# The last four hidden pairs of a feed-forward block by seven block products instead of eight

## The chip, the cores and the metric

The kernel runs on one core of one Trainium2 chip. TensorE (PE) multiplies, VectorE (DVE), ScalarE (ACT) and GpSimd (POOL) work on tiles, SyncE's queue (SP) issues the loads and stores. The metric is the device time of one execution, in microseconds; the time before is the median of three runs.

## The reference

One inference step of an encoder trunk of two layers over 512 prompt frames and 8 x 16 sample frames (640 tokens), width 1024, hidden width 2816, all in float32. Layer 0 is a convolution module and a SwiGLU feed-forward block; layer 1 is banded attention with a shared key/value and a second feed-forward block. The change is in the feed-forward block of layer 0:

```python
def swiglu_ffn(h, g, w_in, w_out):
    a, b = jnp.split(rms_norm(h, g) @ w_in, 2, axis=-1)
    return h + (jax.nn.silu(a) * b) @ w_out
```

The convolution module that comes before it is: RMSNorm, pointwise layer with a gate, causal depthwise convolution of width 31, LayerNorm over the channels, SiLU, pointwise layer (`w_pw2`), added to h.

## The kernel before

**Number format.** Matrix products run in a reduced float32 format in three passes. Every operand is split into `hi` (a ScalarE copy into the reduced format) and `lo` (the remainder, a subtraction), and `mm3` adds `wh*xh + wl*xh + wh*xl` in PSUM, three matmuls for each block of 128 rows. `wsplit` loads a weight tile of up to 128 x 2048 through SP's queue into `raw`, makes `whi` on ScalarE (L156), and `wlo` (L160) on VectorE and GpSimd: its argument `pool` says how many quarters of it GpSimd makes. `raw`, `whi` and `wlo` have two buffers each; every third load has a third raw buffer, `rx`, as long as the pool of that name is open. `xsplit` (L165, L166) splits the moving operand, ScalarE then VectorE.

**Layout.** Activations lie with the features on the partitions: `h` is 128 x 8 x 640. The tokens are in two groups: group 0 has 256 (128 samples and the first 128 prompt frames), group 1 has 384. The hidden width is 22 blocks of 128; a *pair* j is the a-part and the b-part of one of them: `ffn_in` takes 8 blocks x 3 matmuls for each part, 48 matmuls of 256 columns (group 0) or 384 (group 1), then the gate (L293, L294 for group 0, whose input has been normalised beforehand; L296 to L299 for group 1, whose input is only scaled by the gain, with 1/rms, `bca`, multiplied in behind the product), and the split of the hidden rows. `ffn_out` multiplies the hidden rows of a chunk of pairs by `w_out` and adds the result into `h` (L309). With 5 to 8 pairs in the chunk it takes two output tiles to one weight load; with 4 or fewer, four tiles, and it makes all its weights before the first tile. PSUM has four banks for all this (`mm`, L93).

**Order.** Engines work in order; the order of the instructions in each queue is set at build time by a scheduler that simulates the program with priorities (`tc.high_priority` puts splits and gates ahead). For the convolution module the order is written by hand in `PLAN`, a list of steps. Those that matter here: `d101 d127` (VectorE convolves four channel blocks of group 1), `n1` (`conv_ln(1)`, LayerNorm of group 1: column sums by additions on GpSimd, L201, sums over partitions by tiny matmuls, L210, spread again by matmuls, L222), `f` (one chunk of pairs for group 0, as work for PE during the convolution of group 1: chunks 0-5, 6-11, 12-17, with three quarters of each `wlo` on GpSimd), `w1` (the second pointwise layer of group 1, `pw2`), `r1` (`rms_late`: RMSNorm of group 1 for the feed-forward block). After the plan come pairs 18 to 21 for both groups together (`FC`), then pairs 0 to 17 for group 1 (`FD`), and then the attention stage, whose first act is the RMSNorm of `h` for keys and queries.

**The second block.** The feed-forward block of layer 1 computes pairs 3 to 21 by seven block products. The 1024 input features are cut in two halves and the 640 tokens in two halves of 320 (`TH`); the a- and b-weights of a pair then make a 2 x 2 block matrix, and the 2 x 2 product is computed with seven products of blocks (a Strassen-Winograd scheme) instead of eight. A `Unit` is one such pair: `prep` loads and splits four weight blocks and three sums of them (L165/L166, sums at L922, two on VectorE and two on GpSimd, then `prep_back` into `bk`), `m1` to `m7` are the products (`prod`, 12 matmuls of 320 columns each, L977), with additions between them; `xc` holds the seven token blocks (B11, B21, B22 and the sums T1 to T4), split, made once. Units overlap: the next unit's `m1`, `m5`, `m6`, `m2` alternate with this one's `m7`, `m3`, `m4`.

## Time and profile before

| | |
|---|---|
| median of 3 runs | 1541.64 us (1540.84 to 1542.74) |
| profiled execution | 1541.31 us, of which the span of the trace is 1539.5 |
| busy share of the span | PE 95%, VectorE 68%, ScalarE 43%, GpSimd 29% |
| granted TensorE clock, mean | 0.988 |
| data moved | 200.54 MB, mean 130 GB/s |

The profile is of one execution, taken by the hardware profiler. Times in it are us from the span's start. A row of the timeline has start, length, engine, line of the kernel, operation, output<-input, shape and count, and in brackets how long the engine was idle before it and what ended that. A row of grouped instructions has count, total busy time, mean ns of one, and the idle time before them with what ended it. The busy time of a matmul overlaps that of the next: the distance between starts, not the mean of one, is what a matmul costs. PEld is TensorE's weight load, beside the matmuls.

### The profile page before, as it was taken

What the parts mean: (1) busy time and instruction counts of PE and PEld (TensorE: products, weight loads), DVE (VectorE), ACT (ScalarE), POOL (GpSimd) and SP (SyncE); (2) the same over time, 40 slices, a digit from 0 to 9 for tenths busy, and PEclk for the clock granted to TensorE, in tenths of its full rate; (3) what the DMA queues carried; (4) which work ended last, traced back from release to release, by engine and by line L of the source; (5) the groups of instructions that cost most, each with busy time, mean ns of one, the idle gap of its engine ahead of it and who ended that gap; (6) DMA issues with size and microseconds to landing.
All of it is one profiled execution on the core that took longest, in us unless ns stands there. A gap on an engine that the chain in (4) does not pass through costs nothing.

```text
span 1539.5 us, 27212 instructions
## 1 busy us (share of the span) xinstructions
PE 1467.9 (95%) x11054; PEld 1397.9 (91%) x11054; DVE 1049.0 (68%) x1890; ACT 667.1 (43%) x1196; POOL 447.3 (29%) x406
## 2 busy tenths in 40 slices
PE   5988898989999999999999999999999999999998
PEld 5878878988999999999988798896989999999998
DVE  6994999989555444556577767666796467467456
ACT  4544455545423323235455445343564144244144
POOL 6965458987401000001322111110421011011010
PEclk9989899999999999999999999999999999999999
DMA  7884334454421333432555545444103222222222
GB/s 261 249 219 143 123 103 162 146 183 151 151 83 56 123 123 123 126 120 96 196 184 195 170 151 199 150 158 151 32 25 117 76 83 89 76 83 90 76 83 83
DMA packets 57022, 200.54 MB, mean 130 GB/s; under 512 B 10176, under 2 KB 20672, under 8 KB 44096
## 3 DMA queue, kind: packets, MB, share of 16 engines
q1 hardware_dynamic: 56608, 198.48, 39.1%
q8 instruction: 87, 1.43, 0.4%
q10 hardware_dynamic: 288, 0.31, 0.1%
q14 instruction: 39, 0.32, 0.1%
HBM read 187.55 MB, written 11.22 MB: 129 GB/s over the span
## 4 chain that ended last, share of the span: by engine, by line
PE 73%; DVE 15%; issue 3%; ACT 3%; POOL 3%; DMA 3%; SPq 0%; POOLq 0%; ACTq 0%; DVEq 0%
PE mm L176 13%; PE mm L177 13%; PE mm L178 13%; PE pb L977 6%; DVE w L443 4%; PE pc L977 4%; DVE wlo L160 4%; PE pa L977 3%; PE w L803 1%; PE pb L176 1%; PE pb L178 1%; PE pb L177 1%; PE pa L178 1%; PE pa L176 1%; PE pa L177 1%
## 5 line engine op out<-in xcount | busy, mean ns | idle before, releaser
L177 PE MATMUL mm<-x,wlo 128*128 128x256 f32 (+1 forms) x1344 | 417.8, 313 | 15.8 <-DVE wlo L160 15.4
L176 PE MATMUL mm<-x,whi 128*128 128x256 f32 (+1 forms) x1344 | 414.4, 312 | 9.2 <-ACT x L165 6.9
L178 PE MATMUL mm<-x,whi 128*128 128x256 f32 (+1 forms) x1344 | 413.0, 311 | 2.5 <-DVE x L166 2.5
L177 PEld LDWEIGHTS mm<-x,wlo 128*128 128x128 f32 x1344 | 257.1, 191 | 19.4 <-DVE wlo L160 18.3
L176 PEld LDWEIGHTS mm<-x,whi 128*128 128x128 f32 x1344 | 255.1, 191 | 14.1 <-ACT x L165 7.7
L178 PEld LDWEIGHTS mm<-x,whi 128*128 128x128 f32 x1344 | 255.3, 191 | 5.2 <-DVE x L166 4.1
L156 ACT ACTIVATE whi<-raw 128x2048 fp32r<-128x2048 f32 (+2 forms) x87 | 143.9, 1658 | 171.9 <-PE mm L178 105.1
L160 DVE TENSOR_TENSOR wlo<-raw,whi 128x2048 fp32r<-128x2048 f32 (+5 forms) x87 | 156.4, 1801 | 44.7 <-ACT whi L156 44.0
L922 POOL TENSOR_TENSOR raw<-raw 128x512 f32<-128x512 f32 x38 | 56.4, 1485 | 326.4 <-DVE raw L922 255.2
L177 PE MATMUL mm<-hid,wlo 128*128 128x256 f32 (+1 forms) x352 | 107.6, 308 | 6.1 <-DVE wlo L160 6.1
L160 POOL TENSOR_TENSOR wlo<-raw,whi 128x1536 fp32r<-128x1536 f32 (+3 forms) x33 | 93.0, 2822 | 55.1 <-ACT whi L156 55.1
L178 PE MATMUL mm<-hid,whi 128*128 128x256 f32 (+1 forms) x352 | 105.8, 307 | 0.8 <-DVE hid L166 0.7
L443 DVE SCALAR_TENSOR_TENSOR w<-gp,dwv,w 128x384 f32<-128x384 f32 x180 | 104.4, 613 | 0.9
L176 PE MATMUL mm<-hid,whi 128*128 128x256 f32 (+1 forms) x352 | 104.4, 307 | 0.0
L201 POOL TENSOR_TENSOR acc<-sq,sq 128x384 f32<-128x384 f32 (+1 forms) x8 | 8.1, 1006 | 255.8 <-ACT sq L185 255.8
L156 ACT ACTIVATE whi<-rx 128x2048 fp32r<-128x2048 f32 (+1 forms) x30 | 54.0, 1800 | 54.0 <-PE mm L178 42.0
L177 PEld LDWEIGHTS mm<-hid,wlo 128*128 128x128 f32 x352 | 66.0, 188 | 7.1 <-DVE wlo L160 7.1
L160 DVE TENSOR_TENSOR wlo<-rx,whi 128x2048 fp32r<-128x2048 f32 (+4 forms) x30 | 62.9, 2098 | 13.3 <-ACT whi L156 12.4
L423 POOL TENSOR_TENSOR y<-y,cvt 128x256 f32<-128x256 f32 (+1 forms) x60 | 67.9, 1132 | 4.3 <-ACT cvt L422 2.2
L178 PEld LDWEIGHTS mm<-hid,whi 128*128 128x128 f32 x352 | 65.7, 188 | 1.2 <-DVE hid L166 1.2
L176 PEld LDWEIGHTS mm<-hid,whi 128*128 128x128 f32 x352 | 65.1, 188 | 0.3 <-ACT hid L165 0.3
L165 ACT ACTIVATE whi<-raw 128x1024 fp32r<-128x1024 f32 x38 | 39.4, 1054 | 54.2 <-DVE raw L922 19.1
(329 smaller groups left out, 3648.2 us busy)
## 6 DMA issues: line engine op xcount, KB each, us to landing
raw<-in_w_in SPq DMA_DIRECT2D x49, 1024.0 KB
raw<-in_w_out SPq DMA_DIRECT2D x28, 768.0 KB
cache<-in_ck SPq DMA_DIRECT2D x32, 512.0 KB
cache<-in_cv SPq DMA_DIRECT2D x32, 512.0 KB
raw<-in_w_pw SPq DMA_DIRECT2D x14, 1024.0 KB
rx<-in_w_in SPq DMA_DIRECT2D x13, 1024.0 KB
rx<-in_w_pw SPq DMA_DIRECT2D x8, 1024.0 KB
raw<-in_w_kq SPq DMA_DIRECT2D x8, 1024.0 KB
```

Source lines behind the costliest of these rows:

```text
L156: nc.scalar.activation(out=hi[:, a:b], in_=raw[:, a:b], func=AF.Copy)
L160: eng.tensor_tensor(out=lo[:, a:b], in0=raw[:, a:b], in1=hi[:, a:b].bitcast(F32), op=ALU.subtract)
L165: nc.scalar.activation(out=hi, in_=src, func=AF.Copy)
L176: nc.tensor.matmul(ps, wh, xh, start=(i == 0), stop=False)
L177: nc.tensor.matmul(ps, wl, xh, start=False, stop=False)
L178: nc.tensor.matmul(ps, wh, xl, start=False, stop=(i == last))
L201: last["acc"] = eng.tensor_tensor(out=acc[:, :n], in0=prev, in1=s(), op=ALU.add)
L423: nc.gpsimd.tensor_tensor(out=y[g][:, c, :], in0=y[g][:, c, :], in1=pr[:, :n], op=ALU.add)
L443: nc.vector.scalar_tensor_tensor(out=dst, in0=src, scalar=wj, in1=dst, op0=ALU.mult, op1=ALU.add)
L803: nc.tensor.matmul(st[32 * b:32 * b + 32, 0:512], qv[b], KC[b // 2][:, b % 2, :], start=True, stop=True)
L922: ENG[e].tensor_tensor(out=out, in0=a, in1=b, op=op)
L977: nc.tensor.matmul(ps, a[:, c], b[:, k, :], start=(first and k == 0 and i == 0), stop=(k == 3 and i == 2), skip_group_check=not first)
```

## The change

- `FS`, group 0's chunks, become 0-5, 6-11, 12-16 and pair 17 alone. `PLAN` still has three `f`, so pair 17 follows after the plan, and `r1` leaves the plan: `rms_late(1)` is called behind it, and pair 17 of group 0 after it, with three quarters of `wlo` on GpSimd (`PFB` = 3). The three-buffer raw pool (`rxs`) closes before that.
- `rms_late(1, ..., keep=xg)` keeps the scaled rows of group 1 in a tile of their own, `xg`.
- `LE`: the additions of `conv_ln(1)`, for mean and variance, go from GpSimd to VectorE.
- Group 1's pairs 0-5, then the token blocks, then its pairs 6-17, all with `PFB` = 3 (before: `wlo` on VectorE alone). The blocks are made from `xg` in pieces of one feature block (256, 384 or 320 columns): VectorE adds and multiplies, `xsplit` for B11, T1, T2, B21, T3; B22 and T4 are split whole once group 1's operand buffer is free.
- Pairs 18 to 21 come last, for all tokens, as four `Unit`s in one chunk, with the same code as the second block; in this stage their PSUM tiles come from the four `mm` banks in turn. Then `ffn_out` for both groups.
- `Unit`, `prod`, `bank`, `tmp` and the loop (`units`) move up in the file and take the weight source as an argument; the host reorders the b-weights of pairs 18 to 21 as it does for layer 1. A `hook` argument of `ffn` is added and not used by the plan.

```diff
-FS = ((0, 6), (6, 6), (12, 6))
+FS = ((0, 6), (6, 6), (12, 5), (17, 1))
+CHC = 5
-PLAN = ("a0 y ... s1 d101 d127 n1 f f w1 r1")
+PLAN = ("a0 y ... s1 d101 d127 n1 f f w1")
...
-    def rms_late(g, gain, engs=SQ, cut=CUT):
+    def rms_late(g, gain, engs=SQ, cut=CUT, keep=None):
...
-                t = tp.tile([P, 384], F32, tag="n1", name=nm("n1"), bufs=NB1)
+                t = (tp.tile([P, 384], F32, tag="n1", name=nm("n1"), bufs=NB1) if keep is None
+                     else keep[:, k, GR[g][0]:GR[g][0] + n])
...
+    def bank(tag=None):
+        if stage[0] == 0:
+            return mmt()
...
+    LE = (nc.gpsimd, nc.vector)
...
-        r, v = colmean(mu, [lambda c=c: y[g][:, c, :] for c in order], n, LCUT, "mst")
+        r, v = colmean(mu, [lambda c=c: y[g][:, c, :] for c in order], n, LCUT, "mst", LE[g])
...
-        bc, _ = rstd_bc([y[g][:, c, :] for c in order], n)
+        bc, _ = rstd_bc([y[g][:, c, :] for c in order], n, eng=LE[g])
...
-    xs0, xs1 = late[0], late[1]
     cv.close()
+    rxs.close()
+    third[1] = None
...
+    xs0, xs1 = late[0], rms_late(1, V_NFFN, keep=xg)
+    ffn({0: hp0}, w_in0, w_out0, {0: xs0}, (0,), chunks, PFB)
+    hid0.close()
     hid1 = ExitStack()
     hp1 = hid1.enter_context(tc.tile_pool(name="hp1", bufs=1))
-    ffn({0: hp0}, w_in0, w_out0, {0: xs0}, (0,), chunks, PFB)
-    if FC:
-        ffn({0: hp0, 1: hp1}, w_in0, w_out0, {0: xs0, 1: xs1}, (0, 1), FC)
-    ffn({1: hp1}, w_in0, w_out0, {1: xs1}, (1,), FD)
...
+    ffn({1: hp1}, w_in0, w_out0, {1: xs1}, (1,), FD[:1], PFB)
+    for k in range(KT):
+        add("v", xg[:, k, 0:256], xs0[0][:, k, :].bitcast(F32), xs0[1][:, k, :].bitcast(F32))
+        add("v", xg[:, k, 256:640], xg[:, k, 256:640], bca[:, 256:640], ALU.mult)
...
+    def put4(i, src):
+        for k in range(4):
+            xsplit(src[:, k, :], xc[i][0][:, k, :], xc[i][1][:, k, :])
+
+    def sub4(out, a, b):
+        for k in range(4):
+            add("v", out[:, k, :], a[:, k, :], b[:, k, :], ALU.subtract)
+
+    put4(B11, b11)
+    sub4(tq, b12, b11)
+    put4(T1, tq)
+    sub4(tq, b22, tq)
+    put4(T2, tq)
+    put4(B21, b21)
+    sub4(b12, b22, b12)
+    put4(T3, b12)
+    sub4(tq, b21, tq)
+    ffn({1: hp1}, w_in0, w_out0, {1: xs1}, (1,), FD[1:], PFB)
     hid1.close()
...
+    u = Unit(w_in0, FC[0][0], hids[0], 0)
+    u.prep((a22[:, 0:512], a22[:, 512:1024]))
+    with tc.high_priority(offset=HP):
+        put(B22, b22)
+        put(T4, tq)
+    xgs.close()
...
+    u.prep_back()
+    for f in (u.m1, u.m5, u.m6, u.m2):
+        f()
...
+    units(w_in0, range(FC[0][0], FT), pairs(FC), FC, u, hids, hid_c, outs0)
```

More of the change, by code (lines that the diff above doesn't have):

```diff
@@ new lines, in tmp, with add, copy, prod @@
+    def tmp(t):
+        if stage[0] == 0 and t == "t3":
+            t = "n1"
+        return tp.tile([P, 384], F32, tag=t, name=nm(t))[:, 0:HT]
+    def add(e, out, a, b, op=ALU.add):
+        ENG[e].tensor_tensor(out=out, in0=a, in1=b, op=op)
+    def copy(out, src):
+        nc.scalar.activation(out=out, in_=src, func=AF.Copy)
+    def prod(ps, w, x, first):
+        wh, wl = w
+        xh, xl = x
+        for k in range(4):
+            c = slice(k * P, (k + 1) * P)
+            for i, (a, b) in enumerate(((wh, xh), (wl, xh), (wh, xl))):
+                nc.tensor.matmul(ps, a[:, c], b[:, k, :], start=(first and k == 0 and i == 0),
+                                 stop=(k == 3 and i == 2), skip_group_check=not first)
@@ new lines, in put, with units @@
+    def put(i, src):
+        xsplit(src, *xc[i])
+    def units(src, js, where, chunks, u, hids, new_hid, outs):
+        for j in js:
+            c, jj = where[j]
+            w = None
+            if j + 1 < FT:
+                w = Unit(src, j + 1, hids[c], where[j + 1][1])
+                w.prep()
+                w.m1()
+            u.m7()
+            if w:
+                w.m5()
+            u.m3()
+            u.m4()
+            if w:
+                w.m6()
+                w.m2()
+            if jj == chunks[c][1] - 1:
+                outs(c)
+                if w:
+                    hids.append(new_hid())
+                    w.hid = hids[-1]
+            u = w
@@ L339, in tile_trunk, with pairs @@
+    def pairs(chunks):
+        return {j0 + jj: (c, jj) for c, (j0, ch) in enumerate(chunks) for jj in range(ch)}
     hid0 = ExitStack()
@@ L524, in step, with hook @@
     def step(op, arg):
+        if op == "f":
+            def hook(jj):
+                for t in arg.split("."):
+                    if t and int(t[0]) == jj:
+                        step(t[1], t[2:])
+            ffn({0: hp0}, w_in0, w_out0, {0: late[0]}, (0,), (chunks.pop(0),), PFA, hook=hook)
+            return
         g, cs = int(arg[:1] or 0), [int(c) for c in arg[1:]]
@@ L898, in tile_trunk @@
     xg = [xg[:, 0:4], xg[:, 4:8]]
[L899 to L907 removed]
+    stage[0] = 1
     proj_o(NP // 2 - 1)
@@ L1185, in tile_trunk @@
         put(T4, tq)
-    where = {}
-    for c, (j0, ch) in enumerate(F1):
-        for jj in range(ch):
-            where[j0 + jj] = c, jj
     xgs.close()
```

260 lines of the change are left out of this document (127 added, 133 removed).

## The prediction

> **What bounds the kernel now.** I read the page's busy shares first, then a table by stage, then the waits and rows inside the stages that the change touches.
>
> ```profile
> span 1539.5 us, 27212 instructions
> ...
> PE 1467.9 (95%) x11054; PEld 1397.9 (91%) x11054; DVE 1049.0 (68%) x1890; ACT 667.1 (43%) x1196; POOL 447.3 (29%) x406
> ```
>
> Seen over the span PE is the bound. The table by stage (columns: stretch, its length, busy time and count of PE, PEld, DVE, ACT, POOL, then clock, DMA share, GB/s) says where it isn't:
>
> ```profile
> 327.00:386.00 59.00, 53.77 (x463) 52.97 (x463) 50.30 (x56) 29.84 (x40) 46.46 (x22) 1.00 0.48 161
> 386.00:420.00 34.00, 34.00 (x197) 33.74 (x196) 16.64 (x22) 14.94 (x19) 18.01 (x9) 1.00 0.45 155
> ...
> 504.00:730.00 226.00, 225.72 (x1305) 225.40 (x1303) 119.37 (x147) 78.40 (x97) 7.04 (x6) 1.00 0.35 118
> 1349.00:1463.00 114.00, 114.00 (x858) 113.63 (x858) 70.64 (x101) 41.82 (x64) 15.55 (x12) 1.00 0.25 83
> ```
>
> From 207 to 386 three chunks of group 0 (18 pairs) fill PE while VectorE convolves group 1; PE idles for 5.2 of the last chunk's 59 us. From 386 to 730 PE is full: second pointwise layer of group 1 (to 420), the four shared pairs (to 476), their output (to 504), group 1's eighteen pairs (to 730). The last row is a stretch of the second feed-forward block, which already works by seven products, with PE full too. So a microsecond of PE work saved after 386 is a microsecond of time; one moved from before 386 to after it isn't free.
>
> **The saving: four pairs by seven products.** The first two rows are from the chain of waits in the second block (start, length, what), the other two start a group-0 half of successive shared pairs in the timeline:
>
> ```profile
> 1385.05 2.33 PE pa L977 x15
> ...
> 1397.48 2.33 PE pa L977 x15
> ```
>
> ```profile
> 448.93 0.28 PE L176 MATMUL mm<-x,whi 128*128 128x256 f32 x1
> ...
> 462.69 0.28 PE L176 MATMUL mm<-x,whi 128*128 128x256 f32 x1
> ```
>
> A shared pair takes 462.69-448.93 = 13.76 us (48 matmuls of 256 columns and 48 of 384). A unit takes 1397.48-1385.05 = 12.43 us (84 of 320). 4 x 1.33 = 5.3 us gained. The Trainium skill ("TensorE: Matmul & The Clock Gate", section "Wait — 56ns, not 53.3ns?") gives a matmul of N columns N / 2.4 GHz + 2.5 ns; by it the estimate would be 13.04 us a pair, 11.41 us a unit, 6.5 us in all. I stay with the rows, which show the units 1.0 us slower than that.
>
> Per unit VectorE and ScalarE do more than per pair (3584 columns split instead of 2048, four block sums of the weights, two of them on POOL), hidden behind PE in the second block, whose last row above has DVE 62% busy and PE full. The output after the four pairs (476 to 504) is the same work.
>
> **The pair moved back.** Chunk three shrinks from six pairs to five. Its PE work, 48 matmuls of about 0.1135 us (13.76 us less 48 of 226/1305 = 0.173, over 48) plus 24 for its output, is 8.2 us; it comes again after the pointwise layer. What the chunk loses to waiting (5.2 us) goes down by a sixth: about 1.0 us gained. But PE now reaches the pointwise layer 8.2 us earlier, near 378, and its input must be there:
>
> ```profile
> 332.82 3.46 POOL L201 TENSOR_TENSOR acc<-acc,y 128x384 f32<-128x384 f32 x3 [0.16 <-ACT y L446]
> ...
> 349.40 1.03 POOL L201 TENSOR_TENSOR acc<-sq,sq 128x384 f32<-128x384 f32 x1 [1.85 <-ACT sq L185]
> 351.21 3.48 POOL L160 TENSOR_TENSOR wlo<-rx,whi 128x1536 fp32r<-128x1536 f32 x1 [0.78 <-ACT whi L156]
> ...
> 366.36 2.28 POOL L201 TENSOR_TENSOR acc<-acc,sq 128x384 f32<-128x384 f32 x2
> ```
>
> ```profile
> 344.11 3.72 DVE L166 TENSOR_TENSOR hid<-t,hid 128x256 fp32r<-128x256 f32 x1
> ...
> 381.97 1.02 DVE L166 TENSOR_TENSOR x<-n,x 128x384 fp32r<-128x384 f32 x2
> ...
> 393.97 1.03 DVE L166 TENSOR_TENSOR x<-n,x 128x384 fp32r<-128x384 f32 x2 [1.32 <-ACT x L165]
> ```
>
> The normalised group 1 arrives in eight pieces from 383 to 395. The sum of squares before it lasts from 349.4 to 368.6 on POOL, 19.2 us, because four splits like the 3.48 us one stand between seven additions. On VectorE (LE) seven additions at 0.54 (the split of the same shape, half of 1.02-1.03) are 3.8 us, plus waits. VectorE's 128x256 subtraction took 3.72 us where POOL was inside a split (a free one, below, 0.42). With two such waits of 3.5 the sum lasts about 11 us, 8 less than before; the mean's last three additions go the same way (3 x 0.54 for 3.46) and give about 2 more. 10 against the 8.2 needed: no new wait, but no slack. Ends: 2 us gained more, 5 us of waiting (below).
>
> The Trainium skill ("SBUF — State Buffer", section "SBUF: two separate sides") calls the port pair of VectorE and GpSimd an exclusive lock, which a VectorE operation with two SBUF inputs and a GpSimd operation hold against each other for the whole instruction. The 3.72 us row agrees. It speaks against both LE and splitting by POOL during group 1's pairs; my sum has it in as two waits.
>
> **What the moved pair costs where it lands.** It is a chunk of its own: pair 17, then eight output tiles of three matmuls. Weight halves whi/wlo have two buffers. In order of use: pair 17 takes A, output weights of tiles 0-3 B, of 4-7 A, group 1's first pair B. So that pair's weights can be split only when tiles 0-3 are done, and these need the hidden rows of pair 17.
>
> ```profile
> 441.69 0.41 DVE L294 TENSOR_TENSOR t<-t,mm 128x256 f32<-128x256 f32 x1
> 442.59 0.42 DVE L166 TENSOR_TENSOR hid<-t,hid 128x256 fp32r<-128x256 f32 x1 [0.48 <-ACT hid L165]
> ```
>
> ```profile
> L156 ACT ACTIVATE whi<-raw 128x2048 fp32r<-128x2048 f32 x51 | 97.6, 1914 | 98.7 <-PE mm L178 80.9 <-PE pb L178 5.9 <-issue 4.1
> ...
> L160 POOL TENSOR_TENSOR wlo<-raw,whi 128x1536 fp32r<-128x1536 f32 x12 | 43.6, 3634 | 18.0 <-ACT whi L156 18.0
> ```
>
> ```profile
> 343.50 0.69 DVE L160 TENSOR_TENSOR wlo<-raw,whi 128x512 fp32r<-128x512 f32 x1 [1.51 <-ACT whi L156]
> ```
>
> The group of whole-tile splits shows that they wait for PE to free the buffer (80.9 of 98.7 us idle before them). After pair 17's last matmul the hidden rows take 443.01-441.69 = 1.3 us, with 0.1 to hand over 1.4, in which PE has no other work. Then tiles 0-3 (12 x 0.1135 = 1.4), the split (1.91, first quarter on VectorE 0.69, 0.4 of hand-overs) against tiles 4-7 (1.4): 1.6 more. I take 3.0 us lost. Ends: nothing, if hidden rows and weights overlap what is left of the layer before; 6.3, if VectorE's quarter has to wait for POOL's 3.63 us part, as in chunk three:
>
> ```profile
> 326.92 0.39 PE L176 MATMUL mm<-x,whi 128*128 128x256 f32 x2
> 329.17 0.38 PE L177 MATMUL mm<-x,wlo 128*128 128x256 f32 x1 [1.86 <-DVE wlo L160]
> ```
>
> **Group 1's pairs.** Splits go three quarters to POOL (3.63 us, after 1.91 on ACT: 5.6 of the 8.3 us that a pair, 48 x 0.173, gives). Into VectorE's idle time (107 of 226 us) go the token blocks: 16 additions and products of 256 or 384 columns, 16 differences and 20 splits of 320, about 0.5 each, 26 us, then two splits of 1280; ScalarE's 20 copies are as short. They are hidden unless a gate of the last pair of a chunk stands behind a blocked one: 0.5 us over three chunks; ends 0 and 6 (three waits of 3.5 less what other tiles cover). The third raw buffer is closed before these pairs. SP's load of 1 MB is short enough for two: issued at 391.79, its transfer ends by 396.
>
> ```profile
> 391.79 0.33 SPq L145 DMA_DIRECT2D raw<-in_w_in  x1
> ```
>
> ```profile
> 394.00:396.00 2.00, 2.00 (x13) 2.00 (x12) 1.00 (x2) 0.35 (x1) 0.00 (x0) 1.00 0.96 406
> ```
>
> **Entering and leaving the units.** The first unit's weights get their buffer 36 x 0.173 = 6.2 us before PE ends group 1; the chain split, three sums (one on POOL), split is longer. The same start in the second block:
>
> ```profile
> 1139.51 0.38 PE L977 MATMUL pa<-x0f,whi 128*128 128x320 f32 x1 [1.22 <-DVE t L922]
> ...
> 1148.46 0.41 PE L977 MATMUL pc<-x1f,wlo 128*128 128x320 f32 x1 [1.27 <-DVE wlo L166]
> ```
>
> There the blocks were late too; here all but two are long made. I take 1.0; ends 0 and 3.8 (those two and smaller ones). Accumulators come from four banks instead of six; each is read out at least 12 matmuls (1.8 us) before its next use, so nothing. At the end, group 0's last additions now come 16 us (96 matmuls of 0.173) before the next stage, not over 200, so its split and squares share ScalarE and VectorE with the next weights. That entry now costs
>
> ```profile
> 731.02 0.36 PE L176 MATMUL mm<-x,whi 128*128 128x256 f32 x1 [1.30 <-DVE h L309]
> ```
>
> and I add 0.5; ends 0 and 3. Eight more additions into h are hidden.
>
> **Sum.** -5.3 -1.0 +3.0 +0.5 +1.0 +0.5 = -1.3. The profiled execution took 1541.31 (span 1539.5 and 1.8 around it), 0.33 under the median: 1540.0 us, no measurable change (0.2%, about 3.1 us, is what a measurement of this kernel can tell).
>
> **Rivals.**
> - Faster. The waits where the moved pair lands are covered, and the shorter sum of squares takes another 1 us of chunk three's stalls: -5.3 -2.0 +0.8 +0.5+0.5 = -5.5, 1535.8 us. For it: PE took partial tiles of several outputs in the pointwise layer without a stall. Against: with three matmuls to a tile there are no partial tiles. 0.37.
> - Slower, by the port lock as the skill's rule would have it, worked from rows: every one of the four POOL splits between 349 and 369 holds an addition of the chain up for some 3.3 us, the sum lasts 3.8+13 = 17 us, 2 less than before, the mean gives 1.5, and PE, 8.2 us early, waits 4.7 us more: 1544.7 us. It decides once fewer than about 6 us are won on the chain. Against: VectorE often enters first (the 0.69 us row). 0.13.
> - Slower, by the upper end at pair 17 (6.3 for 3.0) with 1.5 for POOL's splits in group 1's chunks: 1544.8 us. 0.10.
> - No measurable change, as summed: 0.40.
>
> Range: 1534.5 to 1546.5, which reaches both sides' cases; the likeliest case alone 1538.2 to 1543.8. Faster 0.37, same 0.40, slower 0.23.
>
> **What would show it.** Units every 12.4 us at the end of the first block; PE at the pointwise layer near 378 with no wait for x; a PE gap of about 1.4 us behind pair 17 and one of 1.6 us before group 1's first wlo; group 1's chunks still 75 us each, PE full; under 1.5 us of gaps around the first unit. It would be wrong if the layer waits for x by more than 2 us, if group 1's pairs wait for POOL's wlo, or if units are longer than 12.6 us.

## The result and the profile after

| | before | after |
|---|---|---|
| median | 1542.19 us (1540.84 to 1546.25, 4 runs) | 1568.14 us (1566.25 to 1572.48, 4 runs) |
| ratio, 95% interval | | 1.0165 (1.0138 to 1.0191) |
| profiled execution, span | 1541.31, 1539.5 | 1566.25, 1564.4 |
| mean granted clock | 0.988 | 0.982 |

The change makes the kernel 26 us slower; 1540.0 was forecast, with 1546.5 as the upper end.

From the page of after, the span and the busy shares:

```profile
span 1564.4 us, 27340 instructions
...
PE 1476.3 (94%) x11006; PEld 1401.6 (90%) x11006; DVE 1116.8 (71%) x1991; ACT 687.9 (44%) x1240; POOL 551.6 (35%) x433
```

PE has 48 matmuls fewer and is busy 8.4 us longer, VectorE has 68 us more and GpSimd 104 us more. The table by stage shows where that hurts (stretch, length, busy time and count of PE, PEld, DVE, ACT, POOL, then clock, DMA share, GB/s):

```profile
330.00:390.00 60.00, 51.13 (x392) 49.31 (x391) 47.49 (x67) 28.86 (x42) 27.61 (x10) 0.91 0.40 132
362.10:368.93 6.83, 6.22 (x29) 6.22 (x30) 3.82 (x5) 1.72 (x3) 3.40 (x2) 0.50 0.48 166
390.00:425.00 35.00, 34.02 (x196) 33.39 (x195) 27.29 (x30) 12.73 (x15) 22.49 (x11) 1.00 0.22 73
425.00:438.00 13.00, 11.54 (x86) 11.35 (x85) 9.23 (x22) 7.96 (x15) 6.79 (x6) 0.87 0.50 170
...
438.00:495.00 57.00, 52.66 (x290) 51.53 (x289) 52.98 (x74) 24.64 (x37) 25.29 (x7) 0.97 0.32 104
...
495.00:670.00 175.00, 174.75 (x1008) 174.39 (x1007) 97.70 (x103) 54.96 (x52) 82.95 (x24) 1.00 0.38 129
670.00:749.00 79.00, 78.36 (x532) 77.41 (x531) 57.01 (x95) 42.05 (x84) 19.07 (x19) 1.00 0.23 81
749.00:764.00 15.00, 10.88 (x72) 10.74 (x71) 8.70 (x18) 5.34 (x13) 5.70 (x8) 0.77 0.42 140
751.30:758.13 6.83, 5.66 (x26) 5.69 (x27) 5.48 (x12) 2.93 (x8) 2.28 (x3) 0.50 0.38 124
```

The rows are, from the top: chunk three (five pairs), 6.8 us inside it, the pointwise layer, pair 17 with its output, group 1's first pairs, the rest of group 1, the units with their output, the exit to the attention stage, 6.8 us inside that. Two things are to be seen. In the stages that lose time the clock is under 1.00, down to 0.50 for 6.8 us at a time; before, the three stages shown between 327 and 730 stood at 1.00. And VectorE, 53% busy in group 1's pairs before (119.37 of 226), is 93% busy in the first of them now (52.98 of 57).

In starts of stages, read off the timelines, before against after: chunk three starts at 326.9 and 330.3; the layer at 386.1 and 390.3 although one pair (8.2 us) is gone; the layer ends at 420.0 and 425.3; pair 17 and its output take 12.9 us for 8.2 us of matmuls; group 1's first six pairs 57.3 against 50.1; its rest the same; the last four pairs with output 78.8 against 84.3; from there to the next projection 14.6 against 9.9. So +5.3 at the end of the layer, +12.9, +7.2, -5.5, +4.7: 24.6 of the 24.9 us between the spans.

The waits behind these numbers, from the timeline of after (start, length, engine, line, operation, tiles, in brackets the idle time and what ended it), first PE, then VectorE, then GpSimd:

```profile
362.71 1.44 PE L211 MATMUL w<-onec,acc 128*128 128x1 f32 x6 [2.78 <-DVE acc L202]
...
380.51 0.39 PE L177 MATMUL mm<-hid,whi 128*128 128x256 f32 x1 [2.27 <-ACT whi L157]
...
432.16 0.49 PE L211 MATMUL w<-onec,acc 128*128 128x1 f32 x3 [1.46 <-POOL acc L202]
...
441.18 0.69 PE L178 MATMUL mm<-x,wlo 128*128 128x384 f32 x1 [2.64 <-DVE wlo L161]
...
752.47 0.55 PE L177 MATMUL mm<-x,whi 128*128 128x256 f32 x1 [2.93 <-DVE rst L233]
...
352.71 0.54 DVE L202 TENSOR_TENSOR acc<-sq,sq 128x384 f32<-128x384 f32 x1
...
356.68 3.85 DVE L202 TENSOR_TENSOR acc<-acc,sq 128x384 f32<-128x384 f32 x1
...
360.79 1.87 DVE L202 TENSOR_TENSOR acc<-acc,sq 128x384 f32<-128x384 f32 x3
...
391.44 6.17 DVE L362 TENSOR_TENSOR xg<-x 128x256 f32<-128x256 f32 x6
...
438.24 2.89 DVE L161 TENSOR_TENSOR wlo<-raw,whi 128x512 fp32r<-128x512 f32 x1
...
749.16 2.70 DVE L167 TENSOR_TENSOR x<-h,x 128x384 fp32r<-128x384 f32 x3
...
356.12 3.99 POOL L161 TENSOR_TENSOR wlo<-rx,whi 128x1536 fp32r<-128x1536 f32 x1 [3.88 <-ACT whi L157]
...
437.12 7.34 POOL L161 TENSOR_TENSOR wlo<-raw,whi 128x1536 fp32r<-128x1536 f32 x2 [2.97 <-ACT whi L157]
```

An addition of 0.54 us takes 3.85 beside GpSimd's split of 3.99; a quarter split, 0.69 us in the kernel before, takes 2.89 beside another one. The first stands in the chain that PE waits 2.78 us for, the second ends the wait of 2.64. The clock falls to half around the waits of over 2 us, and once more around the one of 1.46; the last section says when. The saving itself is there, in the chain of waits:

```profile
673.26 28.00 PE mm L373 x189
```

28.00/189 x 84 = 12.44 us a unit, and no gap ahead of the first one.

### The profile page after: what moved, and what is told of

The parts are those of the page before. It is cut to its first block, busy times and chain, and to the rows that moved or that the text cites. A ratio compares the mean times of both kernels' runs of the same rounds, so it can differ in the third digit from the quotient of the medians.

```text
span 1564.4 us, 27340 instructions
## 1 busy us (share of the span) xinstructions
PE 1476.3 (94%) x11006; PEld 1401.6 (90%) x11006; DVE 1116.8 (71%) x1991; ACT 687.9 (44%) x1240; POOL 551.6 (35%) x433
## 4 chain that ended last, share of the span: by engine, by line
PE 66%; DVE 19%; issue 4%; DMA 4%; POOL 3%; ACT 3%; SPq 0%; POOLq 0%; ACTq 0%; DVEq 0%
PE mm L177 10%; PE mm L178 10%; PE mm L179 10%; PE pb L373 6%; DVE wlo L161 5%; DVE w L597 5%; PE pc L373 4%; PE pa L373 3%; PE mm L373 3%; PE w L1032 1%; ACT whi L157 1%; PE pb L177 1%; PE pb L178 1%; PE pb L179 1%; PE pa L179 1%
## 5 line engine op out<-in xcount | busy, mean ns | idle before, releaser
L177 PE MATMUL mm<-x,whi 128*128 128x256 f32 (+1 forms) x1216 | 378.1, 315 | 11.8 <-ACT x L166 6.4
L179 PE MATMUL mm<-x,whi 128*128 128x256 f32 (+1 forms) x1216 | 377.0, 313 | 3.4 <-DVE x L167 3.3
L161 POOL TENSOR_TENSOR wlo<-raw,whi 128x1536 fp32r<-128x1536 f32 (+5 forms) x66 | 203.2, 3081 | 196.0 <-ACT whi L157 196.0
L177 PEld LDWEIGHTS mm<-x,whi 128*128 128x128 f32 x1216 | 233.2, 193 | 17.0 <-ACT x L166 7.6
L179 PEld LDWEIGHTS mm<-x,whi 128*128 128x128 f32 x1216 | 233.2, 193 | 6.3 <-DVE x L167 5.1
L157 ACT ACTIVATE whi<-raw 128x2048 fp32r<-128x2048 f32 (+3 forms) x98 | 160.0, 1636 | 157.5 <-PE mm L179 93.6
L161 DVE TENSOR_TENSOR wlo<-raw,whi 128x512 fp32r<-128x512 f32 (+7 forms) x98 | 151.0, 1544 | 47.6 <-ACT whi L157 47.3
L166 ACT ACTIVATE whi<-raw 128x1024 fp32r<-128x1024 f32 x46 | 47.7, 1054 | 64.1 <-DVE raw L362 28.2
L167 DVE TENSOR_TENSOR hid<-t,hid 128x256 fp32r<-128x256 f32 (+1 forms) x36 | 68.1, 1891 | 0.6 <-ACT hid L166 0.6
L167 DVE TENSOR_TENSOR wlo<-raw,whi 128x1024 fp32r<-128x1024 f32 x46 | 59.7, 1311 | 10.2 <-ACT whi L166 9.6
L373 PE MATMUL pa<-x0f,whi 128*128 128x320 f32 x228 | 60.1, 311 | 3.2 <-ACT whi L166 1.2
L177 PEld LDWEIGHTS mm<-hid,whi 128*128 128x128 f32 x288 | 54.8, 193 | 6.1 <-ACT whi L157 5.1
L149 ACT ACTIVATE whi<-raw,vec 128x128 fp32r<-128x128 f32 (+1 forms) x160 | 52.5, 411 | 17.4 <-PE mm L179 15.8
```

The costliest lines, as they stand in the source:

```text
L149: nc.scalar.activation(out=hi[:, a:b], in_=raw[:, a:b], func=AF.Copy, scale=gain)
L157: nc.scalar.activation(out=hi[:, a:b], in_=raw[:, a:b], func=AF.Copy)
L161: eng.tensor_tensor(out=lo[:, a:b], in0=raw[:, a:b], in1=hi[:, a:b].bitcast(F32), op=ALU.subtract)
L166: nc.scalar.activation(out=hi, in_=src, func=AF.Copy)
L167: nc.vector.tensor_tensor(out=lo, in0=src, in1=hi.bitcast(F32), op=ALU.subtract)
L177: nc.tensor.matmul(ps, wh, xh, start=(i == 0), stop=False)
```

## The experiments

Three theories stood against each other. **Contention**: VectorE is late around the layer and at the exit, because GpSimd's splits hold it up and the token blocks and LayerNorm additions stand in its queue. **Order**: with four pairs moved to the end, too little PE work lies behind the layer, and group 0's output too close to the exit, whatever VectorE does. **Products**: the units cost more than they save. The stage table puts the third aside; the runs below bear on the first two. Each ratio is against the kernel before on the same chip; runs on different chips are better compared by it than by their medians. Stage times and waits are from one profiled execution of each version, which can lie some us from its median (7 in e15_pl2, where it is the longest of twelve).

**LayerNorm's additions back on GpSimd** (e1_le_pool).

```diff
-    LE = (nc.gpsimd, nc.vector)
+    LE = (nc.gpsimd, nc.gpsimd)
```

> The changed kernel with the LayerNorm additions of group 1 back on GpSimd (LE = gpsimd, gpsimd), all else as changed. Theory A (the additions on VectorE cost: TensorE's column-sum matmul stands 2.8 us behind them, then runs 4 us at half clock, so 5 us): about 1563 us, no TensorE wait on 'acc' near 362 and the second pointwise layer some 5 us earlier than 390. Rival B (the additions are innocent; the layer is late because chunk three is one pair shorter and its splits are late): 1567 to 1572 us, since the sum on GpSimd is longer still and TensorE now waits for x at the layer.

Measured: 1561.18 us, ratio 1.0132 (1.0098 to 1.0166), 7 us less. Chunk three starts at 327.0 and PE is at the layer at 378.2, but the layer takes 40.2 us instead of 34. The layer by the table, and a wait in the timeline:

```profile
378.00:418.00 40.00, 34.93 (x194) 33.30 (x194) 30.77 (x40) 17.91 (x24) 19.69 (x11) 1.00 0.21 68
```

```profile
401.78 0.45 PE L178 MATMUL mm<-x,wlo 128*128 128x384 f32 x1 [2.84 <-DVE wlo L161]
```

`LE` costs 7 us between the medians and 6.9 at the end of the layer, through chunk three, though the two intervals overlap. At the layer some 6 us are then lost, which fits the shorter chunk: what it saves is waited for.

**No pair behind the layer** (e2_six).

```diff
-FS = ((0, 6), (6, 6), (12, 5), (17, 1))
+FS = ((0, 6), (6, 6), (12, 6))
```

> The changed kernel with pair 17 back in chunk three (FS = 0-5, 6-11, 12-17). Theory A (pair 17 as a chunk of its own costs 4.7 us more than its work, and TensorE comes too early to the pointwise layer): 1558 to 1562 us, and the layer starts near 398 with no gap. Rival B (what pair 17 covers, the split of group 1's rows for the feed-forward block, is now bare): a gap of 6 to 10 us behind the layer, then 3 us of half clock, 1566 to 1572 us.

Measured: 1574.77 us, 1.0220 (1.0195 to 1.0245). The layer starts at 399.1; layer and group 1's first six pairs take 107.7 us, where they took 104.9 with pair 17 between them. Not one gap of 6 to 10 us, as rival B had it, but six waits of 1.6 to 3.1 lie in it. In this order the pair behind the layer covers more than it costs.

**VectorE alone makes `wlo` behind the plan** (e3_pfb0).

```diff
-PFB = 3
+PFB = 0
```

> The changed kernel with the low halves of the weights of pair 17 and of group 1's pairs on VectorE alone again (PFB = 0). Theory A (GpSimd's part of the split, during which VectorE's two-input operations stand still, makes the first pairs of group 1 slow): the 2.6 us wait for wlo at 441 and the 1.4 us wait for a bank at 461 go, with their half clock, about 1561 us. Rival B (VectorE is full with the token blocks there, whoever splits): within 2 us of the changed kernel, 1565 to 1569 us, the first chunk of group 1 still 57 us long.

Measured: 1568.63 us, 1.0166 (1.0133 to 1.0200): nothing. The wait for `wlo` gives way to one of 2.95 us at 443.5 for VectorE's addition of an output tile into `h`, and the first six pairs still take 56.2 us. That spoke for the rival; two runs further down (e14_mid_pfb0, e17_spread_pfb0) say otherwise.

**Token blocks held back, and spread.** One run (e4_hold) lets them start only behind the gate of pair 5, one (e5_spread, with `LE` on GpSimd) issues four pieces per pair behind a pair's gate:

```diff
+    held = ExitStack()
+    held.enter_context(tc.issue_after(last["gate"].ins))
...
+    held.close()
```

> The changed kernel with one ordering edge: VectorE begins the token blocks only behind the last gate of group 1's pair 5 (about 25 us of work, out of the LayerNorm chain and of the first chunk of group 1, into the 150 us behind it). Theory A (the blocks, pulled forward by the scheduler, hold up x of the pointwise layer at 391 to 398 and the evictions and splits of group 1's first pairs): 2 us less before 425 and 5 us less between 438 and 495, about 1561 us. Rival B (they only fill gaps that the port lock leaves): 1566 to 1569 us.

```diff
+    def hook(jj):
+        pairs_done[0] += 1
+        if pairs_done[0] > 1:
+            with tc.issue_after(last["gate"].ins):
+                for _ in range(4):
+                    next(todo, None)
...
+    ffn({1: hp1}, w_in0, w_out0, {1: xs1}, (1,), FD, PFB, hook=hook)
```

> The changed kernel with two edits: the LayerNorm additions of group 1 back on GpSimd, and the token blocks made four VectorE pieces at a time, each four behind the gate of one of group 1's pairs (from the second pair on), so that they neither run ahead into the pointwise layer nor in a burst. Theory A (burst and LayerNorm additions are separate costs and add up): 7 us less from the LayerNorm additions, 6 to 8 us less in group 1's first chunk (50 to 52 us instead of 57) and no burst at an output: about 1553 us. Rival B (any block work on VectorE between those pairs costs about its own time in TensorE waits): 1559 to 1562 us, as with the LayerNorm additions alone.

Measured: held 1575.58 us, 1.0226 (1.0185 to 1.0267): the first chunk's pairs come down to 51.7 us, but its output takes 35.3 instead of 25.1, with waits of 4.10 and 2.07 us: the burst only moved, and neither expectation came. Spread 1558.75 us, 1.0097 (1.0075 to 1.0120), 2.4 less than with `LE` alone, which these runs do not resolve. Group 1's first six pairs take 55.5 us, not the 50 to 52 of theory A: a wait of 3.44 us for `wlo` at 438.4 stays. The layer takes 41.0, the exit is unchanged.

**The order alone** (e6_plain_last): the same order with plain pairs 18 to 21 last, no units, no token blocks, `LE` on GpSimd.

```diff
-    xs0, xs1 = late[0], rms_late(1, V_NFFN, keep=xg)
+    xs0, xs1 = late[0], rms_late(1, V_NFFN)
...
+    ffn({1: hp1}, w_in0, w_out0, {1: xs1}, (1,), FD, PFB)
+    ffn({0: hp0, 1: hp1}, w_in0, w_out0, {0: xs0, 1: xs1}, (0, 1), FC)
```

> The order of the changed kernel without its products: the LayerNorm additions on GpSimd, pair 17 behind the pointwise layer, group 1's pairs, then pairs 18 to 21 last for both groups by plain pairs of 48 matmuls a group, no token blocks. Theory A (the new order by itself costs: about 6 us at the pointwise layer that TensorE now reaches before x, 3 to 5 around pair 17, 5 at the entry to the attention stage, and the products win 5 to 6): 1555 to 1558 us. Rival B (the order is free, the losses are the blocks' and the products'): 1541 to 1545 us.

Measured: 1565.39 us, 1.0153 (1.0118 to 1.0188). Pair 17 with its output, group 1's first pairs and the last pairs by the table, then the waits before the first pair's `wlo` and at the exit, with VectorE's and GpSimd's splits ahead of the first:

```profile
421.00:436.00 15.00, 12.38 (x83) 12.01 (x82) 12.47 (x26) 8.18 (x15) 4.41 (x5) 0.77 0.42 142
436.00:493.00 57.00, 53.54 (x294) 53.23 (x293) 37.98 (x31) 16.51 (x18) 26.35 (x7) 0.94 0.35 115
...
669.00:752.00 83.00, 83.00 (x581) 83.00 (x579) 42.70 (x74) 32.33 (x65) 10.01 (x12) 1.00 0.22 75
```

```profile
440.35 0.69 PE L178 MATMUL mm<-x,wlo 128*128 128x384 f32 x1 [3.46 <-DVE wlo L161]
...
755.22 0.36 PE L177 MATMUL mm<-x,whi 128*128 128x256 f32 x1 [2.92 <-DVE rst L233]
...
436.87 7.28 DVE L161 TENSOR_TENSOR wlo<-raw,whi 128x512 fp32r<-128x512 f32 x2
...
436.30 7.30 POOL L161 TENSOR_TENSOR wlo<-raw,whi 128x1536 fp32r<-128x1536 f32 x2 [5.52 <-ACT whi L157]
```

The order as made, with GpSimd's splits in it, costs some 23 us with no block product at all; the units win some 5 back (82.9 us for the plain pairs and their output against 78.5 in e5_spread; 6.6 between the medians), and the token blocks cost little once they are spread. Without any token block, and with VectorE 67% busy, group 1's first six pairs still take 56.8 us: there VectorE's two quarter splits last 7.28 us beside GpSimd's 7.30.

**Group 1's part of the last output ahead of group 0's** (e7_spread_out10, on e5_spread).

```diff
-                                 for g in range(2)}, (0, 1), 0)
+                                 for g in range(2)}, (1, 0), 0)
```

> As the kernel with spread blocks, and the output behind the units takes group 1 before group 0. Theory A (the attention stage starts 5 us late because the RMSNorms of both groups and the split of group 1 crowd VectorE behind the last output tiles; with group 1 first its longer norm lies under group 0's 11 us of output): 2 to 3 us less than that kernel. Rival B (the first projection needs group 0, whose rows are now the last to come): 0 to 4 us more.

Measured: 1561.03 us, 1.0120 (1.0093 to 1.0147); two waits of 2.89 and 1.19 become five, the longest 5.61 for GpSimd's sum of squares. No gain.

**The price of a wait by itself** (e8_idle): the kernel before, with PE made to wait twice between group 1's chunks, nothing else changed.

```diff
-    ffn({1: hp1}, w_in0, w_out0, {1: xs1}, (1,), FD)
+    for n_idle, ck in zip((0, 1, 3), FD):
...
+            for _ in range(n_idle):
+                nc.gpsimd.tensor_tensor(out=junk, in0=src, in1=src, op=ALU.add)
...
+            stop = nc.tensor.matmul(sink[:, 0:P], ident, junk[:, 0:P], start=True, stop=True)
+            hold = tc.issue_after(stop.ins)
```

> The kernel before with two waits put between group 1's three chunks, where TensorE is otherwise full: a tiny matmul behind the last addition into h and one GpSimd addition (TensorE idle some 2.2 us), at the next boundary three additions (some 4.5 us), and all later matmuls kept behind it. Theory A (a wait of 2 us or more costs more than itself, since TensorE then runs some 4 us at half clock): the granted clock is 0.5 for 3 to 4 us behind the waits, and the time is 2 x 2 us more than the two waits: about 1552 us. Rival B (half clock in the changed kernel has another cause): clock 1.0 behind the waits, 1548 us.

Measured: 1553.52 us, 1.0072 (1.0049 to 1.0095). The two waits, and the stretches behind them:

```profile
580.92 0.49 PE L576 MATMUL w<-junk,ident 128*128 128x128 f32 x2 [1.56 <-POOL junk L573]
...
662.23 0.58 PE L576 MATMUL w<-junk,ident 128*128 128x128 f32 x1 [5.36 <-POOL junk L573]
```

```profile
580.90:583.00 2.10, 2.08 (x13) 2.08 (x13) 1.65 (x1) 0.41 (x1) 0.00 (x0) 1.00 0.28 117
662.20:664.00 1.80, 1.77 (x6) 1.77 (x7) 0.00 (x0) 0.00 (x0) 0.00 (x0) 0.50 0.86 209
664.00:666.00 2.00, 2.00 (x7) 2.00 (x7) 0.00 (x0) 0.00 (x0) 0.00 (x0) 0.51 0.80 336
666.00:668.00 2.00, 2.00 (x13) 2.00 (x13) 0.00 (x0) 0.00 (x0) 0.00 (x0) 1.00 0.00 0
```

The wait of 1.56 us leaves the clock at 1.00 and the next six pairs at 50.55 us (50.09 before); the one of 5.36 is followed by 3.8 us at half clock and 52.06 us for the pairs.

**Buffers of its own for pair 17's output weights** (e9_own, on e5_spread).

```diff
-            ws.append(wsplit(src, ch * mg, P, parts=mg, pool=pool))
+            ws.append(wsplit(src, ch * mg, P, parts=mg, pool=pool, own=own))
...
+    op_ = op_s.enter_context(tc.tile_pool(name="op", bufs=2))
```

> e5_spread with buffers of their own (two sets of 128x128 pieces for a weight's float32, high and low parts) for the output weights of pair 17, so that group 1's first pair need not stand behind them in the shared weight buffers. In e5_spread TensorE waited 3.44 us at 438.4 us for that pair's low part. Theory A (the wait is the order of the weight buffers): the wait falls under 1 us, the half granted clock behind it goes too, and the time is some 5 to 6 us under e5_spread's 1558.75 us, near 1553. Theory B (VectorE and POOL are late whatever buffer is used, since the split itself runs in the shadow of POOL's work): a wait of over 2 us for the low part stays, and the time lies within 2 us of e5_spread.

Measured: 1557.37 us, 1.0103 (1.0077 to 1.0128). Group 1's first pairs now take 50.5 us, so the wait for `wlo` goes, as theory A has it; but pair 17 and its output take 17.3 us, so the time is theory B's, within 2 us of e5_spread. PE's row, then two of VectorE:

```profile
426.94 0.58 PE L183 MATMUL mm<-hid,ohi 128*128 128x256 f32 x1 [3.65 <-ACT hid L172]
...
417.50 4.05 DVE L167 TENSOR_TENSOR wlo<-raw,whi 128x512 fp32r<-128x512 f32 x1 [0.93 <-ACT whi L163]
421.47 4.63 DVE L173 TENSOR_TENSOR x<-xg,x 128x384 fp32r<-128x384 f32 x8
```

VectorE stands 4.05 us in a quarter split and 4.63 in group 1's operand before it comes to the gate that PE waits for. It isn't the buffers.

**Pair 18 behind the layer, chunk three with six pairs, three units** (e10_pair18, on e9_own); **then the last splits at the exit held back** (e11_pair18_exit).

```diff
-FS = ((0, 6), (6, 6), (12, 5), (17, 1))
-FC = ((18, 4),)
-FD = ((0, 6), (6, 6), (12, 6))
+FS = ((0, 6), (6, 6), (12, 6), (18, 1))
+FC = ((19, 3),)
+FD = ((0, 6), (6, 6), (12, 4), (16, 3))
```

> e9_own, and the third chunk of group 0 keeps its six pairs: the pair behind the pointwise layer is number 18, and three products of units remain instead of four. Theory A (a chunk of five pairs brings TensorE to the layer before VectorE has the layer's inputs ready, at a cost of some 6.5 us): the layer starts near 386 us and takes about 34 us as before the change, and the time is about 5 us under e9_own, the unit fewer costing 1.3. Theory B (the layer's waits come from what stands on VectorE during the layer itself, not from when TensorE arrives): the layer takes 40 us again, and the time is e9_own's within 1.5 us, or above it.

```diff
+        with tc.issue_after(hold.ins) if hold else ExitStack():
             nc.vector.tensor_tensor(out=lo, in0=src, in1=hi.bitcast(F32), op=ALU.subtract)
```

> e10_pair18, and at the exit VectorE makes the last two low parts of group 1's values for the next projection only behind the last addition to the residual, so that the PSUM banks come free earlier. Theory A (the 2.9 us wait for a bank at about 752 us in the changed kernel, with the half clock behind it, comes from subtractions that POOL slowed ahead of that addition): the wait falls under 1.5 us and the time is 3 to 4 us under e10_pair18. Theory B (the bank waits for the addition itself, which POOL's squares slow as much): within 1 us of e10_pair18.

Measured: 1558.74 us, 1.0114 (1.0083 to 1.0145), and 1560.99 us, 1.0135 (1.0097 to 1.0173). The layer takes 36.2 us when it is reached later, against 37.2 in e9_own: in this version the shortened chunk is 1 us of it. (The step from 41.0 to 37.2 came with the buffers, before the chunk was changed.) 17.5 us for one pair and its output stay. At the exit a wait of 2.69 us for ScalarE's next weights takes the place of 3.22 for the bank. Both expectations of a gain failed.

**Two pairs behind the layer** (e12_two, on e10_pair18); **then the units ahead of group 1's last chunk** (e13_mid; that chunk is pairs 14 to 19, since two units are left; the token blocks come five pieces to a pair, and the units' buffer `bk` has one copy); **then `PFB` = 0 in that version** (e14_mid_pfb0).

```diff
-FS = ((0, 6), (6, 6), (12, 6), (18, 1))
-FC = ((19, 3),)
+FS = ((0, 6), (6, 6), (12, 6), (18, 2))
+FC = ((20, 2),)
```

> e10_pair18 with two pairs (18 and 19) of group 0 behind the pointwise layer instead of one, two products of units left, and only the first half of their output weights in a buffer of its own. Theory A (the work behind the layer is too short to cover the sum over the partitions, the hidden rows and the next split: in e10_pair18 one pair and its output took 17.5 us from 419.7 us on for 8.2 us of matmuls): the 9 us lost there shrink to about 3, the unit fewer costs 1.3, and the time is 4 to 6 us under e10_pair18's 1558.74 us, near 1553.5. Theory B (VectorE has a backlog that must be worked off behind the layer however much is put there): 7 us or more are lost there again, and the time is 1558 us or more.

```diff
+    ffn({1: hp1}, w_in0, w_out0, {1: xs1}, (1,), FD[:-1], PFB, hook=hook)
...
     fcs.close()
+    ffn({1: hp1}, w_in0, w_out0, {1: xs1}, (1,), FD[-1:], PFB)
```

> e12_two with the units moved ahead of the last chunk of group 1 (pairs 14 to 17), so that group 1's own output is the last work before the attention stage, as in the kernel before. Theory A (the exit costs more because group 0's last additions, squares and splits now lie within 17 us of the next stage): the wait of 2.9 us and its half clock at the exit go back to the 1.3 us of the kernel before, some 4.5 us, against up to 1.5 us for one more change of weights between the units and the chunk: 3 to 4.5 us under e12_two. Theory B (the exit is late for VectorE's and ScalarE's work on the next weights, whatever comes last): a wait of over 2.5 us stays, and the time is e12_two's within 1.5 us, or above it.

```diff
-PFB = 3
+PFB = 0
```

> e13_mid with PFB = 0: behind the plan every low part of the weights is made by VectorE alone. Theory A (the split shared with GpSimd is what makes VectorE late: in e13_mid its quarter of a split took 4.04 us beside GpSimd's 3.50, where VectorE made a whole one in 2.29 in the kernel before; behind the layer two pairs and their output took 25.1 us for 16.4 us of matmuls, and at the exit the last quarter took 3.07 us): the pairs behind the layer take 20 us or less, the wait at the exit falls from 3.13 to under 2 us, and the time is 7 to 10 us under e13_mid's 1559.4 us, near 1551. Theory B (VectorE has too much to do in these two places whoever makes the low parts; without the split on GpSimd the change itself did not get faster): within 3 us of e13_mid.

Measured: 1567.31 us, 1.0165 (1.0143 to 1.0188); 1559.38, 1.0112 (1.0088 to 1.0135); 1547.51, 1.0047 (1.0029 to 1.0065). Two pairs behind the layer, expected to win 4 to 6 us, come out 8.6 slower (0.5% by the ratios): 8.3 us are lost there (24.7 for 16.4 of matmuls), as against 9.3 with one, so it is not the length of the cover. The exit took 18.4 us in that run, with waits of 3.80 and 2.84 for GpSimd. With the units ahead of group 1's last chunk these 8 us come back, which is more than expected, but the time is only that of e10_pair18 again, and the exit still waits 3.13 us. Taking GpSimd's splits out is worth 12 us by the medians and 10 by the ratios (the two ran on different chips), where 7 to 10 were expected. The version with the units moved ahead (e13_mid): the pairs behind the layer and the exit by the table, then one split and the exit's wait in the timeline:

```profile
424.00:449.00 25.00, 21.04 (x157) 19.95 (x157) 19.77 (x25) 10.14 (x17) 12.03 (x6) 0.93 0.42 142
...
743.00:757.00 14.00, 9.68 (x60) 9.43 (x59) 8.68 (x19) 5.68 (x15) 4.45 (x6) 0.76 0.44 150
```

```profile
417.82 4.04 DVE L167 TENSOR_TENSOR wlo<-raw,whi 128x512 fp32r<-128x512 f32 x1 [0.93 <-ACT whi L163]
...
732.26 3.07 DVE L167 TENSOR_TENSOR wlo<-raw,whi 128x384 fp32r<-128x384 f32 x1 [0.67 <-POOL acc L208]
...
746.32 0.55 PE L183 MATMUL mm<-x,whi 128*128 128x256 f32 x1 [3.13 <-DVE h L318]
...
417.81 3.50 POOL L167 TENSOR_TENSOR wlo<-raw,whi 128x1536 fp32r<-128x1536 f32 x1 [3.63 <-ACT whi L163]
```

The same with `PFB` = 0:

```profile
422.00:443.00 21.00, 19.44 (x160) 18.83 (x159) 15.52 (x25) 10.26 (x17) 2.08 (x2) 1.00 0.45 151
...
736.00:745.00 9.00, 6.92 (x60) 6.87 (x61) 6.04 (x16) 4.05 (x10) 4.40 (x6) 1.00 0.69 233
```

```profile
416.15 2.29 DVE L167 TENSOR_TENSOR wlo<-raw,whi 128x2048 fp32r<-128x2048 f32 x1 [0.94 <-ACT whi L163]
...
736.89 0.36 PE L183 MATMUL mm<-x,whi 128*128 128x256 f32 x1 [1.01 <-ACT whi L155]
```

VectorE makes the whole `wlo` in 2.29 us, and its quarter in 4.04 when GpSimd makes the rest: giving three quarters away costs VectorE 1.75 us. Pairs and output go from 25 to 21 us, the exit from 14.5 to 9.2 (9.9 in the kernel before), the clock in both to 1.00.

**What is left at the layer**, on e14_mid_pfb0: its own splits on VectorE alone (e15_pl2); and, instead, no separate buffer for the two pairs' output weights (e16_noown).

```diff
-PL2 = (2, 2)
+PL2 = (2, 0)
```

> e14_mid_pfb0, and the low parts of the second pointwise layer's weights for group 1 are made by VectorE alone too (before and so far half of each by GpSimd). In e14_mid_pfb0 the layer takes 38.2 us, 4.3 more than in the kernel before, with a wait of 2.54 us at 404.3 us for a low part whose VectorE half took 2.02 us and stood behind a scaling of 2.03 us (0.41 beside an idle GpSimd). Theory A (these are slow beside GpSimd's splits): the wait goes, the layer takes 34 to 36 us, and the time is 2 to 4 us under e14_mid_pfb0's 1547.5 us. Theory B (VectorE, which makes the layer's inputs at the same time, has no time for the other halves): the layer waits for x instead, and the time is the same within 1.5 us or longer.

```diff
-    ffn({0: hp0}, w_in0, w_out0, {0: xs0}, (0,), chunks, PFB, own=op_)
+    ffn({0: hp0}, w_in0, w_out0, {0: xs0}, (0,), chunks, PFB)
```

> e14_mid_pfb0 without the buffer of its own for the output weights of the two pairs, so that they are split after the layer and not during it (in e14_mid_pfb0 ScalarE's 1.06 us and VectorE's 1.23 us for them stand ahead of the split that TensorE waits 2.54 us for at 404.3 us). Theory A (that split comes late because of them): the wait falls under 1 us, the layer takes 34 to 36 us, and the time is 2 to 4 us under e14_mid_pfb0's 1547.5 us, less what comes back at the output. Theory B (the wait is GpSimd's): the layer stays within 1 us of 38.2 us, and the time is the same or longer.

Measured: 1545.93 us, 1.0025 (1.0012 to 1.0037), and 1546.90, 1.0036 (1.0023 to 1.0048). The layer takes 35.5 and 34.6 us instead of 38.2. The stage of the second version:

```profile
385.00:420.00 35.00, 34.55 (x199) 33.97 (x198) 21.73 (x28) 15.07 (x20) 18.02 (x9) 1.00 0.33 111
```

The first edit brings the layer's wait from 2.54 us down to 1.74, the second takes it away, but gives part back in group 1's first pairs (51.7 us for 50.1). In ratios they are worth 0.2% and 0.1%, at the edge of what these runs resolve. The first is the best version found, and it is still 0.25% behind the kernel before.

**GpSimd's splits taken out of the change's own order** (e5_spread, with one pair behind the layer and four units last), without and with the layer's (e17_spread_pfb0, e18_spread_dve).

```diff
-PFB = 3
+PFB = 0
```

> e5_spread (the change with GpSimd's additions in the LayerNorm and the token blocks spread over the pairs) with PFB = 0: the order of the change, one pair behind the layer and four units last, without GpSimd's part of the splits behind the plan. Theory A (these splits are the main cause in the change itself, not only in the rebuilt order of e13_mid): the wait of 3.44 us at 438.4 us and that of 2.89 us at the exit fall under 1.5 us each with their half clock, and the time is 7 to 11 us under e5_spread's 1558.75 us, near 1550. Theory B (the change's order is the cause, and GpSimd's splits only where two pairs stand behind the layer): within 3 us of e5_spread.

```diff
-PL2 = (2, 2)
+PL2 = (2, 0)
```

> e17_spread_pfb0, and the low parts of the second pointwise layer's weights for group 1 by VectorE alone, as in e15_pl2, where that was worth 1.6 us. Theory A (the layer's waits are GpSimd's): the layer, 41.0 us in e5_spread, takes 37 us or less and the time is 2 to 4 us under e17_spread_pfb0, near the kernel before. Theory B (the layer waits for x, which a VectorE with more to do makes later): the layer takes 40 us or more and the time is e17_spread_pfb0's within 1.5 us, or above it.

Measured: 1554.85 us, 1.0073 (1.0057 to 1.0089), and 1557.33, 1.0093 (1.0079 to 1.0107). So 3.9 us, between the two theories, and with intervals that overlap those of e5_spread. The wait for `wlo` goes down to one of 2.20 for ScalarE's part, the exit's stays at 2.92, the layer's at 2.10 for x (40.6 us). With the layer's splits on VectorE as well the layer still takes 38.9, now waiting 2.68 us for `wlo` at its start: no gain. With GpSimd's splits out, e14_mid_pfb0 to e16_noown lie at 1.0047 to 1.0025 and this order at 1.0073 and 1.0093, so the order costs time whoever makes the splits. Here the layer is reached before VectorE has its inputs, and at the exit VectorE's three splits of group 1's x (2.69 us at 741.26, 2.70 in the changed kernel) stand ahead of the last addition into `h` and of what PE waits for, with or without GpSimd's splits.

## Why the prediction was wrong

Taken by its own terms.

**Units, -5.3: right.** 84.3 us became 78.8, -5.5, at 12.44 us a unit. The entry to them, +1.0, cost nothing.

**Chunk three, -1.0, and "no new wait": wrong, the largest miss.** The length of the chain was right: the sum of squares runs from 352.71 to 362.66, 10 us for the 11 forecast. What failed is the step from there to PE. The sums over partitions are matmuls, and they stand in PE's own queue between the pairs: PE waited 2.78 us for the chain instead of running ahead of it, and then ran 6.2 us at half clock. Other things came late too (the chunk's start, +3.3 us; 2.27 at the output, for a ScalarE copy that stood behind one waiting for VectorE); with the additions on GpSimd neither is there. PE reached the layer at 390.3, not near 378. With the additions back on GpSimd it was there at 378.2, as worked out, and the layer gave the time back (40.2 us). With one pair less PE should have been 9.2 us ahead at the end of the layer; it was 5.3 us behind, 14.5 us off. Without `LE` the layer ended at 418.3, 1.7 us ahead: `LE` is 7 of the 14.5, and 7.5 are lost without it, some 6 of them at the layer. So "10 against the 8.2 needed" fails with the additions on either engine.

**Pair 17 where it lands, +3.0, and group 1's pairs, +0.5: mis-sized.** The stage of pair 17 lost 4.7 us and group 1's first six pairs 7.2, together 11.9 for 3.5. The places were right (behind pair 17, then the first `wlo`), though what PE waited 1.46 us for behind pair 17 was GpSimd's sum of squares for group 1's RMSNorm, which the sum did not have. At `wlo` the reason of the upper end came: VectorE's quarter behind GpSimd's part, enough by itself (e6_plain_last, 56.8 us without a token block). The other step that failed is the one that put the token blocks "into VectorE's idle time (107 of 226 us)": that is an average over eighteen pairs, and the scheduler put the blocks into the first six, where VectorE is 93% busy. Held out of there (e4_hold), the six pairs take 51.7 us, but the next output pays for it. How much of the 7.2 us is the blocks' in the change itself was not separated. Six additions for them also came ahead of two of the layer's inputs (6.17 us at 391.44); PE lost 0.51 us there.

**Exit, +0.5: mis-sized**, +4.7, above the end of 3 given for it. Two causes, each enough by itself: with the output of both groups last, the wait is 2.92 us without GpSimd's splits (e17_spread_pfb0); with group 1's chunk last and GpSimd's splits it is 3.13 (e13_mid); only without both is it 1.01 (e14_mid_pfb0).

**What no term held: the clock behind a wait.** Mean clock times span says 18.5 us were lost to it before (1539.5 x 0.012) and 28.2 after (1564.4 x 0.018): 9.7 of the 24.9 us. That counts idle time at half clock as lost too; half of the time that PE was busy in these stretches is 14.1 us before and 21.6 after, 7.5 us more. The prediction counted every wait at its own length.

**The rivals.** The port lock was put on the LayerNorm chain, where it held one addition up (3.85 us) and decided little. The same rule, the exclusive lock of the Trainium skill ("SBUF — State Buffer", section "SBUF: two separate sides"), decided elsewhere: the trace agrees with it in 4.04 us for a quarter split beside GpSimd's 3.50. By it the quarter, 0.69 us free, comes behind the 3.50: an estimate of 4.2 us, against 2.29 for the whole split on VectorE alone, so that a shared split saves VectorE nothing. The rival had counted four such splits inside the sum of squares; the rows before the change show three between its additions, and the fourth only behind the last of them. The faster rival needed the waits around pair 17 to be covered, and they were not.

**What is shown and what stays open.** `LE` costs 7 us (one version, intervals that overlap). GpSimd's splits behind the plan cost nothing that can be seen in the change itself, 4 us in its order with `LE` on GpSimd and the blocks spread (not resolved), and 10 to 12 with two pairs behind the layer and the units ahead of group 1's last chunk. The order with GpSimd's splits costs some 23 us without units or blocks. So neither contention nor order explains the 26 us alone. The rebuilt order with the splits in stands at 1.0112, the change's order with the splits out at 1.0073, and both together at 1.0047 to 1.0025 (the rebuilt versions also have two units instead of four). How the order's part divides between the shortened chunk, the single pair behind the layer and the output of both groups at the end stays open; the versions that changed one of them (six pairs, pair 18, two pairs, group 1's output first) did not get faster while GpSimd's splits were there, and only moving the units ahead did, against a version that had just lost as much. How much of the last 3.7 us of the best version lies at the layer and how much in the entry to the two units was not separated.

## What to carry to other kernels

When PE work is moved, look at what VectorE does in the stage it leaves and in the one it enters, not at its share of the span, and follow tiny matmuls in PE's queue as consumers of VectorE's chain. A split shared between VectorE and GpSimd is to be costed as the time that VectorE is blocked: here the whole on VectorE took 2.29 us and a quarter beside GpSimd 4.04. Before a wait is taken away, ask what stands behind it on the late engine: in several of these runs (e3_pfb0, e4_hold, e9_own, e11_pair18_exit) the wait only moved.
